# A two-layer diffusion block on one core: five weight fetches behind the softening, and a first chunk's columns ahead of the second half of its turning

## The chip, the cores and the metric

The kernel runs on one core of a Trainium2 chip. Five engines of that core take part, each with its own queue of instructions: TensorE (PE in the profile; PEld are its weight loads), VectorE (DVE), ScalarE (ACT), GpSimd (POOL) and SyncE (SP, which only starts transfers here). They wait for each other through semaphores. The metric is the device time of one execution in microseconds (us), lower is better.

## The reference

Two layers act on 256 latent tokens (`x`) and 256 context tokens (`ctx`) of width 1024, in 32-bit floats. Every layer computes shifts, scales and gates from two condition vectors, mixes the tokens, normalizes, and applies a squared-ReLU MLP of width 4096. Layer 0 mixes by retention with four heads, layer 1 by attention with 32 heads of 32 channels: a latent token attends to a window of 4 rows by 16 columns of latent tokens, with a bias for each head, and to all context tokens.

```python
for i in range(DEPTH):
    mod = (silu_c @ ada_w[i] + ada_b[i])[:, None, :]
    sh1, sc1, g1, sh2, sc2, g2 = jnp.split(mod, 6, axis=-1)
    h = x * (1.0 + sc1) + sh1              # and hc from ctx
    y, yc = retention_mixer(...) if i % 2 == 0 else neighbourhood_mixer(...)
    x = layer_norm(DN_ALPHA * x + g1 * y, ...)
    x = layer_norm(DN_ALPHA * x + g2 * sq_relu_mlp(x * (1.0 + sc2) + sh2, ...), ...)
...
s = jnp.concatenate([s_loc + bias, s_ctx], axis=-1)      # in neighbourhood_mixer
prob = jax.nn.softmax(s, axis=-1)
```

## The kernel before

Matrix products keep more than one rounding's accuracy: an operand is split into a high part (`hi`, a cast on ACT) and a low part (`lo`, the difference, on DVE), and a product is the sum of three passes on PE: high by high, high by low and low by high. `fetch(n)` starts the transfer of the next n weight blocks (128x1024 each, 512 KB, into four `raw` buffers) and casts their high part on ACT; `lows(n)` forms the low parts that are still owed on DVE. `take(n)` hands the next blocks to a product. Five `hi` and five `lo` buffers go round.

In the two places that the change touches, the order of PE, ACT and DVE is the order in which the program is written (all three are "in program order" there), so an instruction that waits holds up all that stands behind it on its engine. All instructions are recorded by one helper, so nearly every row of the profile names line 84, and work is told apart by the names of its tiles.

**The start.** Layer 0's first projections run chunk by chunk over the eight 128-wide slices of the model width. For a chunk, `chunk_sums` multiplies the condition weights (`rawq`) into one bank of the accumulator memory, `prs` (`pada` in the profile), `chunk_row` copies the sums out (`row`), `chunk_columns` turns them into columns (written to `pada` again) from which DVE makes the shifts and scales (`mod`), `chunk_turn` transposes the four token tiles (`R`), and `chunk_modulate` applies `mod` and writes `hTh` and `hTl`, the operand of the projections (`pq`, `pv`). `turn_over(n)` issues n products of a constant tile (`still`) whose result nobody uses.

**The attention of layer 1.** Thirteen steps n = 0 to 12, each of which works on three groups of four heads at once, follow a table, `STEPS`, with one row (early, late, last, before, after) for each:

```python
for n, (early, late, last, before, after) in enumerate(STEPS):
    gather(n + 1); turned(n)
    fetch(early); lows(early)
    scores(n + 2); soften(n + 2)
    fetch(late); lows(late)
    run(before)
    flip(n + 1); invert(n + 2); fetch(last); attend(n)
    run(after)
```

(here with several calls to a line). `scores` is 12 products on PE into four banks (`pqk`). `soften` adds the bias and takes the minimum on DVE (`s`, `mn`, shown as ISA or CUSTOM_DVE), four instructions, and ACT follows with four exponentials (`s<-s,mn`). `before` is a projection of later heads: `K(g)` for keys (`pn`, evicted to `kT` by ACT and then DVE), `Q(2)` for queries (`pn`, evicted to `qT`), `V(t)` for values (`pnv`). `V(0)` takes four weight blocks and goes through them in order, 6 of its 24 products for each block. `flip` is 13 transposes (`ppt`), copied out by ACT and DVE in turn (`pt`). `attend` is 26 products into `pav`, which DVE multiplies with the inverted sums (`rt`) and ACT and DVE split (`oTh`, `oTl`). `turned` is a copy of a part of `pav` to `rt` on ACT. GpSimd copies a corner (`gather`) and starts the bias transfers of two steps later.

Of the kernel before, what the change touches and what calls it, by code (L numbers as in the profile page):

```python
# [104 lines left out]
def kernel(  # L105
# [46 lines left out]
    def nm(s):  # L152
        uid[0] += 1
        return f"{s}_{uid[0]}"

    def bank(s="ps"):
        return psp.tile([P, 512], F32, tag="ps", name=nm(s))
# [8 lines left out]
    def tsl(t):  # L166
        return slice(t * P, (t + 1) * P)
# [613 lines left out]
    class Weights:  # L781


        Q, V = slice(0, DK), slice(DK, DK + DV)
# [22 lines left out]
    def turn_over(n):  # L807
        for _ in range(n):
            pe.matmul(pq[0][:, :256], lhsT=still[:, :P], rhs=still[:, :256], start=True, stop=True)
# [42 lines left out]
    prs, pts, rows = {}, {}, {}  # L852
# [16 lines left out]
    def chunk_row(k, cols=slice(0, 2 * P)):  # L869
        if cols.start == 0:  # L870
            rows[k] = smp.tile([P, 256], F32, tag="row", name=nm("row"), bufs=1)
        dve.tensor_copy(out=rows[k][:, cols], in_=prs[k][:, cols])

    def chunk_columns(k):
        for i in range(2):
            pe.matmul(
                prs[k][:, 2 * i : 2 * i + 2], lhsT=rows[k][:, tsl(i)], rhs=cv("sel4")[:, 0:2],
                start=True, stop=True,
            )
        dve.tensor_add(  # L880
            out=mods[0, 0][:, :, k, :],
            in0=prs[k][:, 0:4].rearrange("p (s t) -> p s t", s=2),
            in1=bcol[:, :, k].unsqueeze(2).broadcast_to([P, 2, 2]),
        )

    KINDS = slice(0, NLAT), slice(NLAT, NT)

    def chunk_turn(k):

        pts[k] = bank("pt")[:, 0:256], prs[k][:, 256:512]  # L890
        for t in range(4):
            pe.transpose(pts[k][t // 2][:, tsl(t % 2)], R[t][:, tsl(k)], ident)

    def modulated(e, out_ap, pt, k, a):
# [47 lines left out]
    turn_over(3)  # L942
    chunk_sums(0, 1)
    chunk_row(0, tsl(1))
    chunk_turn(0)
    chunk_columns(0)
    turn_over(4)
    w = ws[0]
    w.high(w.Q)
    chunk_modulate(0, lambda: (w.high(w.V), w.low(w.Q)))  # L950
# [6 lines left out]
    for k in range(KC):  # L957
# [10 lines left out]
        if k < KC - 1:  # L968
            for i in range(2):
                chunk_sums(k + 1, i)  # L970
            chunk_turn(k + 1)
            ws[k + 1].high()
            chunk_row(k + 1)
            if k > 2:
                ws[k + 1].low()
# [69 lines left out]
    for h in range(RH):  # L1045
# [13 lines left out]
        else:  # L1059
# [7 lines left out]
            for u in range(4):  # L1067
                ((wh, wl),) = take(1)
                for t in range(4):
                    for kk in range(2):  # L1070
                        k = 2 * u + kk
# [431 lines left out]
    def q_pair(p):  # L1503
        for u in range(2):
            q_mm(p, u)
        q_evac(p)
# [20 lines left out]
    def k_part(g, a=0, b=NT):  # L1527
        k_evac(k_mm(g, a, b), g, a, b)
# [11 lines left out]
    def v_part(half, t):  # L1540
        if t == 0:
            vu[0] = take(4, 0)
        ps = bank("pnv")
        for k in range(KC):
            wh, wl = vu[0][k // 2]
            mm3(ps[:], hs(k, t * P, (t + 1) * P), (wh[:, k % 2, :], wl[:, k % 2, :]), k == 0, k == KC - 1)
        act.copy(out=vtile(t, half), in_=ps[:])
# [28 lines left out]
    sums, rrs, Es, pts, pss = {}, {}, {}, {}, {}  # L1576
# [245 lines left out]
    def K(g):  # L1822
        return lambda: k_part(g)

    def Q(p):
        return lambda: q_pair(p)

    def V(t):
        return lambda: v_part(1, t)

    def W(half, t):
# [7 lines left out]
    REST = lambda: rest_evac(rest_mm(1))  # L1839
    STEPS = [  # L1840
        (1, 0, 0, [K(2)], []),
        (2, 0, 0, [K(3)], []),
        (2, 0, 0, [K(4)], []),
        (1, 0, 0, [K(5)], []),
        (2, 0, 0, [Q(2)], []),
        (1, 1, 0, [V(0)], []),
        (0, 0, 0, [V(1)], []),
        (0, 0, 0, [V(2)], [REST]),
        (0, 0, 0, [V(3)], []),
# [399 lines left out]
```

## Time and profile before

| what | value |
|---|---|
| median of 3 runs | 1186.27 us (1185.79 to 1186.78) |
| profiled execution | 1188.31 us, of which span 1186.5 us |
| PE busy | 1176.7 us, 99% of the span |
| DVE busy | 832.8 us, 70% |
| ACT busy | 480.9 us, 41% |
| POOL busy | 248.9 us, 21% |
| transfers | 193.16 MB, mean 163 GB/s |

The profile is of one execution; its engines' busy shares are averages over stages with different limits. PE's 99% counts a product as busy until its modelled end, so short waits inside a stage show only in the rows of that stage. The start takes the first 10 us, the steps of the attention lie between 848 and 960 us.

### The profile page before, as it was taken

To read this page: it belongs to the slowest core of one execution; us is meant where nothing else is said; L and a number is where in the kernel's file an instruction comes from. 1 tells how busy PE (TensorE), PEld (TensorE's weight loads), DVE (VectorE), ACT (ScalarE), POOL (GpSimd) and SP (SyncE) were. 2 spreads that over 40 slices of the span, in tenths; PEclk is the share of its full clock that TensorE was granted. 3 is DMA by queue.
4 is the path that set the end of the run, shared out by engine and by line. 5 is a ranking of instruction groups with operands and counts; after the bars stand their busy time and mean duration, and the time that the engine had idled before them with its cause. 6 is when DMAs were issued, how large, how long until landed. Compare 5 with 4: busy or idle time off the path is not lost.

```text
span 1186.5 us, 17867 instructions
## 1 busy us (share of the span) xinstructions
PE 1176.7 (99%) x6884; PEld 990.9 (84%) x6884; DVE 832.8 (70%) x1304; ACT 480.9 (41%) x813; POOL 248.9 (21%) x389
## 2 busy tenths in 40 slices
PE   9999999999999999999999999999999999999997
PEld 7778888888888889888888888889888878999886
DVE  3876975886688487757876675668467588876446
ACT  3652222322223246441212333137466666665341
POOL 0104301310330141780202000223344430000001
PEclk9999999999999999999999999999999999999999
DMA  9964441444254216756566665637244434765660
GB/s 276 273 234 161 142 158 56 143 130 137 89 160 160 77 55 209 203 112 215 177 193 211 200 213 185 206 108 215 69 143 125 118 122 152 224 201 185 227 212 36
DMA packets 138041, 193.16 MB, mean 163 GB/s; under 512 B 9772, under 2 KB 81108, under 8 KB 137956
## 3 DMA queue, kind: packets, MB, share of 16 engines
q1 hardware_dynamic: 129572, 179.02, 47.3%
q0 software_dynamic: 7232, 10.44, 3.9%
q10 hardware_dynamic: 1152, 2.56, 0.7%
q8 instruction: 54, 0.88, 0.3%
q14 instruction: 31, 0.25, 0.1%
HBM read 187.15 MB, written 5.75 MB: 163 GB/s over the span
## 4 chain that ended last, share of the span: by engine, by line
PE 96%; ACT 1%; DVE 1%; issue 1%; DMA 0%; POOL 0%; DVEq 0%; ACTq 0%
PE p L84 44%; PE pq L84 8%; PE pg L84 7%; PE pv L84 7%; PE pw L84 7%; PE pn L84 5%; PE pnv L84 4%; PE po L84 3%; PE pada L84 2%; PE pnw L84 1%; PE pS L84 1%; PE ppt L84 1%; PE pqk L84 1%; PE pt L84 1%; PE pav L84 1%; PE p1t L84 1%
## 5 line engine op out<-in xcount | busy, mean ns | idle before, releaser
L84 ACT CAST hi<-raw 128x1024 fp32r<-128x1024 f32 (+2 forms) x228 | 232.7, 1032 | 325.0 <-PE p L84 151.3
L84 DVE TENSOR_TENSOR lo<-raw,hi 128x1024 fp32r<-128x1024 f32 (+2 forms) x228 | 280.3, 1240 | 101.8 <-ACT hi L84 101.0
L84 PE MATMUL p<-hi,hid 128*128 128x512 f32 (+1 forms) x832 | 241.8, 374 | 0.0
L84 PEld LDWEIGHTS p<-hi,hid 128*128 128x128 f32 x832 | 152.1, 188 | 27.7
L84 PE MATMUL p<-hTh,lo 128*128 128x256 f32 (+1 forms) x512 | 166.9, 329 | 0.0
L84 PE MATMUL p<-hTl,hi 128*128 128x256 f32 (+1 forms) x512 | 166.9, 329 | 0.0
L84 PE MATMUL p<-hTh,hi 128*128 128x256 f32 (+1 forms) x512 | 164.0, 330 | 0.0
L84 PE MATMUL p<-lo,hid 128*128 128x512 f32 (+1 forms) x416 | 155.3, 373 | 0.0
L84 DVE SCALAR_TENSOR_TENSOR acc<-rawa,scol,acc 128x1024 f32<-128x1024 f32 x56 | 74.7, 1344 | 63.1 <-DMA rawa<-in_ada_w_dram 62.9
L84 POOL TENSOR_TENSOR R<-R,acc 128x512 f32<-128x512 f32 x40 | 62.2, 1565 | 212.3 <-DVE acc L84 212.2
L84 PEld LDWEIGHTS p<-hTl,hi 128*128 128x128 f32 x512 | 96.4, 188 | 8.7
L84 PEld LDWEIGHTS p<-hTh,lo 128*128 128x128 f32 x512 | 96.3, 188 | 8.8
L84 PEld LDWEIGHTS p<-hTh,hi 128*128 128x128 f32 x512 | 95.1, 190 | 8.7
L84 PEld LDWEIGHTS p<-lo,hid 128*128 128x128 f32 x416 | 78.4, 188 | 13.6
L84 ACT CAST hid<-r 128x256 fp32r<-128x256 f32 (+1 forms) x64 | 31.9, 500 | 103.4 <-DVE r L84 103.3
L84 DVE SCALAR_TENSOR_TENSOR strips<-rawa,scol,strips 128x512 f32<-128x512 f32 x84 | 66.4, 847 | 0.0
L84 POOL TENSOR_TENSOR rstd<-rstd,misc 128x1 f32<-128x1 f32 x28 | 19.2, 686 | 215.5 <-DVE rstd L84 214.3
L84 ACT ACTIVATE s<-s,mn 128x512 f32<-128x512 f32 x64 | 45.5, 712 | 26.2 <-DVE mn L84 26.1
L84 PE MATMUL pg<-hi,hTh 128*128 128x512 f32 x128 | 51.1, 399 | 0.0
L84 PE MATMUL pw<-hi,oh 128*128 128x512 f32 x128 | 50.9, 398 | 0.0
L84 PE MATMUL pg<-lo,hTh 128*128 128x512 f32 x128 | 50.0, 391 | 0.0
L84 PE MATMUL pw<-hi,ol 128*128 128x512 f32 x128 | 50.0, 390 | 0.0
(238 smaller groups left out, 2277.1 us busy)
## 6 DMA issues: line engine op xcount, KB each, us to landing
raw<-in_mlp_w_dram SPq DMA_DIRECT2D x128, 512.0 KB, 4.2
rawa<-in_ada_w_dram SPq DMA_DIRECT2D x80, 512.0 KB, 4.3
raw<-in_ret_w_in_dram SPq DMA_DIRECT2D x42, 512.0 KB, 3.6
raw<-in_nat_w_in_dram SPq DMA_DIRECT2D x24, 512.0 KB, 3.9
rawq<-in_ada_w_dram SPq DMA_DIRECT2D x16, 512.0 KB, 5.8
raw<-in_ret_w_o_dram SPq DMA_DIRECT2D x16, 512.0 KB, 4.4
bias<-rpb_rows POOLq DMA_DIRECT2D x32, 128.0 KB, 2.9
raw<-in_nat_w_o_dram SPq DMA_DIRECT2D x8, 512.0 KB, 4.1
```

The source lines that it names most:

```text
L84: r = f(*args, **kwargs)
```

## The change

In the first chunk, the second pair of the transposes (context tokens, `R_105`) goes into a bank of its own instead of the second half of `prs`, and stands behind `chunk_columns`; one of the four idle products behind it is dropped. In steps 1 to 5 of the attention, the blocks that `fetch(early)` and `lows(early)` handled ahead of the softening are handled by `fetch(late)` and `lows(late)` behind it. Step 5 had one block on either side; now both are behind. The number of blocks in each step, and every product, stay the same.

```diff
-    def chunk_turn(k):
+    def chunk_turn(k, ts=range(4)):
 
-        pts[k] = bank("pt")[:, 0:256], prs[k][:, 256:512]
-        for t in range(4):
+        if k not in pts:
+            pts[k] = bank("pt")[:, 0:256], (prs[k][:, 256:512] if k else bank("pt")[:, 0:256])
+        for t in ts:
             pe.transpose(pts[k][t // 2][:, tsl(t % 2)], R[t][:, tsl(k)], ident)
...
-    chunk_turn(0)
+    chunk_turn(0, (0, 1))
     chunk_columns(0)
-    turn_over(4)
+    chunk_turn(0, (2, 3))
+    turn_over(3)
...
         (1, 0, 0, [K(2)], []),
-        (2, 0, 0, [K(3)], []),
-        (2, 0, 0, [K(4)], []),
-        (1, 0, 0, [K(5)], []),
-        (2, 0, 0, [Q(2)], []),
-        (1, 1, 0, [V(0)], []),
+        (0, 2, 0, [K(3)], []),
+        (0, 2, 0, [K(4)], []),
+        (0, 1, 0, [K(5)], []),
+        (0, 2, 0, [Q(2)], []),
+        (0, 2, 0, [V(0)], []),
         (0, 0, 0, [V(1)], []),
```

PE at the start of the program, around the first chunk's columns (`pada_177<-cst_81,row_186`; `cst_81` holds the identity):

```order
 L84 MATMUL pada_177<-rawq_121,cT 32x128 x8
 L84 MATMUL pt_205<-cst_81,R_104 128x128 x2
-L84 MATMUL pada_177<-cst_81,R_105 128x128 x2
 L84 MATMUL pada_177<-cst_81,row_186 128x2 x2
-L84 MATMUL pq_116<-still_95 128x256 x4
+L84 MATMUL pt_206<-cst_81,R_105 128x128 x2
+L84 MATMUL pq_116<-still_95 128x256 x3
 L84 MATMUL pq_116<-hTh,hi_217 128x512
```

The columns moved ahead of the second pair of transposes, whose result is now `pt_206`.

ACT in step 5 (`oTh_6957<-rt_7687` ends step 4; the four ACTIVATE are the exponentials; the two casts are the high parts of the last block of `V(0)` and of the first block of `Q(3)`), before:

```order
L84 CAST oTh_6957<-rt_7687 128x4x32
L84 COPY rt_7834<-pav_6956 128x128
L84 CAST hi_7838<-raw_7836 128x1024
L84 ACTIVATE s_7860,sums_7859<-s_7860,mn_7858 128x512
L84 ACTIVATE s_7863,sums_7859<-s_7863,mn_7858 128x512
L84 ACTIVATE s_7866,sums_7859<-s_7866,mn_7858 128x512
L84 ACTIVATE s_7869,sums_7859<-s_7869,mn_7858 128x512
L84 CAST hi_7874<-raw_7872 128x1024
```

and of the change:

```order
L84 CAST oTh_6957<-rt_7687 128x4x32
L84 COPY rt_7834<-pav_6956 128x128
L84 ACTIVATE s_7854,sums_7853<-s_7854,mn_7852 128x512
L84 ACTIVATE s_7857,sums_7853<-s_7857,mn_7852 128x512
L84 ACTIVATE s_7860,sums_7853<-s_7860,mn_7852 128x512
L84 ACTIVATE s_7863,sums_7853<-s_7863,mn_7852 128x512
L84 CAST hi_7868<-raw_7866 128x1024
L84 CAST hi_7873<-raw_7871 128x1024
```

The high part of `V(0)`'s last block (`hi_7838`, now `hi_7868`) went from ahead of the four exponentials to behind them.

DVE behind the softening of step 4, where two blocks are handled and the queries are evicted (`qT`), before:

```order
L84 ISA s_7728,mn_7717<-pqk_7704,bias_6872 128x512
L84 ISA mn_7717 128x1
L84 SCALAR_TENSOR_TENSOR qT_6611<-pn_7731,qT_6611 128x256
L84 SCALAR_TENSOR_TENSOR qT_6611<-pn_7732,qT_6611 128x256
L84 COPY pt_6960<-ppt_7790 128x384
```

and of the change:

```order
L84 ISA mn_7705 128x1
L84 TENSOR_TENSOR lo_7722<-raw_7719,hi_7721 128x1024
L84 TENSOR_TENSOR lo_7727<-raw_7724,hi_7726 128x1024
L84 SCALAR_TENSOR_TENSOR qT_6611<-pn_7731,qT_6611 128x256
L84 SCALAR_TENSOR_TENSOR qT_6611<-pn_7732,qT_6611 128x256
L84 COPY pt_6960<-ppt_7790 128x384
```

The two low parts now stand between the softening and the eviction of the projection, and no longer ahead of the softening.

## The prediction

> **What bounds the kernel now.** I read the page first, then the chain of work that ended last in order of time around the attention's steps, then the rows of DVE, ACT and PE there, and last the first 30 us.
>
> ```profile
> span 1186.5 us, 17867 instructions
> ...
> PE 96%; ACT 1%; DVE 1%; issue 1%; DMA 0%; POOL 0%; DVEq 0%; ACTq 0%
> ```
>
> PE carries 96% of the chain, so only work that makes PE wait can be worth time. In the steps it does wait. In the chain the columns are start, length and what:
>
> ```profile
> 857.69 0.90 PE pqk L84 x10
> 858.59 5.67 PE pn L84 x24
> ...
> 875.93 0.47 ACT kT L84
> 876.40 0.38 ACT pt L84
> ...
> 876.82 1.31 PE pqk L84 x9
> ...
> 883.84 1.42 PE ppt L84 x13
> 885.26 1.12 PE pav L84 x27
> 886.39 1.28 PE pqk L84 x12
> 887.67 5.95 PE pn L84 x48
> ...
> 896.16 1.64 PE pqk L84 x11
> ...
> 906.02 1.53 PE pqk L84 x11
> ...
> 915.77 0.90 PE pqk L84 x9
> ```
>
> A step in which PE waits for nothing is 0.90 scores + 5.67 projection + 1.42 transposes + 1.12 attend = 9.11 us. Step 1 starts at 857.69, so without a wait step 3's scores would start at 875.91 and last 0.90, to 876.81. They ended at 876.82 + 1.31 = 878.13: 1.32 lost by then. In steps 4, 5 and 6 the scores took 1.28, 1.64 and 1.53 in place of 0.90: 0.38, 0.74 and 0.63 lost. From 915.77 on (step 7) nothing is. All that the steps can give is therefore 1.32 + 0.38 + 0.74 + 0.63 = 3.07 us, 0.26% of the whole. What held the scores back is a bank that ACT and DVE had not emptied (ACT's `kT` and `pt` stand right ahead in the chain), so the loop through these two engines was longer than PE's 9.11.
>
> **That loop, before and after.** DVE's rows (start, length, what), then ACT's:
>
> ```profile
> 858.53 0.29 DVE L84 TENSOR_TENSOR oTl<-rt,oTh 128x128 fp32r<-128x128 f32 x1 [0.37 <-ACT oTh L84]
> ...
> 866.14 0.69 DVE L84 TENSOR_TENSOR kT<-pn,kT 128x512 fp32r<-128x512 f32 x1 [1.70 <-ACT kT L84]
> 866.75 1.15 DVE L84 COPY pt<-ppt 128x384 f32<-128x384 f32 x2
> ...
> 868.88 0.29 DVE L84 TENSOR_TENSOR oTl<-rt,oTh 128x128 fp32r<-128x128 f32 x1 [0.37 <-ACT oTh L84]
> 869.99 2.36 DVE L84 TENSOR_TENSOR lo<-raw,hi 128x1024 fp32r<-128x1024 f32 x2 [0.82 <-ACT hi L84]
> ...
> 876.43 0.69 DVE L84 TENSOR_TENSOR kT<-pn,kT 128x512 fp32r<-128x512 f32 x1 [1.63 <-ACT kT L84]
> ...
> 896.04 0.75 DVE L84 SCALAR_TENSOR_TENSOR qT<-pn,qT 128x256 fp32r<-128x256 f32 x2 [1.44 <-ACT qT L84]
> 896.71 1.14 DVE L84 COPY pt<-ppt 128x384 f32<-128x384 f32 x2
> ...
> 905.72 1.23 DVE L84 TENSOR_TENSOR lo<-raw,hi 128x1024 fp32r<-128x1024 f32 x1 [2.10 <-ACT hi L84]
> 906.86 1.15 DVE L84 COPY pt<-ppt 128x384 f32<-128x384 f32 x2
> ...
> 908.99 0.29 DVE L84 TENSOR_TENSOR oTl<-rt,oTh 128x128 fp32r<-128x128 f32 x1 [0.37 <-ACT oTh L84]
> 909.30 0.69 DVE L84 CUSTOM_DVE_ANT_1 s<-pqk,bias 128x512 f32<-128x512 f32 x1
> ```
>
> ```profile
> 868.91 2.00 ACT L84 CAST hi<-raw 128x1024 fp32r<-128x1024 f32 x2
> ...
> 901.82 0.73 ACT L84 ACTIVATE s<-s,mn 128x512 f32<-128x512 f32 x1 [1.90 <-DVE mn L84]
> ...
> 904.66 1.03 ACT L84 CAST hi<-raw 128x1024 fp32r<-128x1024 f32 x1
> ...
> 910.04 0.72 ACT L84 ACTIVATE s<-s,mn 128x512 f32<-128x512 f32 x1 [0.92 <-DVE mn L84]
> ```
>
> Before, a round with two blocks took 876.43 - 866.14 = 10.29 us. The change reorders it; each link is a distance of two starts above. From the keys' eviction to `oTl`: 868.88 - 866.14 = 2.74. From `oTl` to a softening that stands right behind it: 909.30 - 908.99 = 0.31. From there to the first exponential: 910.04 - 909.30 = 0.74. Four exponentials: 904.66 - 901.82 = 2.84. From a cast to its low part: 905.72 - 904.66 = 1.06. A low part, to the next on DVE: 906.86 - 905.72 = 1.14. The second cast adds nothing, since two take 2.00 and its low part has to wait for the first one anyway. So a round with two blocks becomes 2.74 + 0.31 + 0.74 + 2.84 + 1.06 + 2 x 1.14 = 9.97, and with one block 8.83. The work is the same; it is only 0.32 shorter, because the casts, which DVE waited for ahead of the softening, now stand behind the exponentials, and DVE waits for them there.
>
> Rounds after the change, from the `oTl` of 858.53, which lies ahead of the first moved row: softening at 858.84; the keys' eviction of step 1 at 858.84 + 6.92 = 865.76 (before 866.14); step 2 at + 9.97 = 875.73 (before 876.43); step 3, one block, at + 8.83 = 884.56; the queries' eviction of step 4 at + 9.97 = 894.53 (before 896.04). PE follows: steps 2 to 4 run nearly at 9.11, and the banks turn so that the scores of step 3 no longer wait for the keys' bank. In step 5 two of the four banks still come from `qT`, whose pair takes 0.75: 894.53 + 0.75 = 895.28, then nine score products of 0.90 / 12 each, and `V(0)` starts near 896.0, against 896.16 + 1.64 = 897.80. So some 1.8 of the 2.44 lost ahead of it come back.
>
> **Where it is given back.** `V(0)`'s last block (products 19 to 24) was cast ahead of the softening; now it is cast behind step 5's exponentials, in the very step that uses it. Its low part: 894.53, eviction to `oTl` 2.74 + 0.06 (the queries' pair takes 896.71 - 896.04 = 0.67 where the keys take 866.75 - 866.14 = 0.61), softening at 897.64, cast 0.74 + 2.84 later at 901.22, low part 902.28 to 903.51 (1.23). PE before:
>
> ```profile
> 902.17 0.39 PE L84 MATMUL pnv<-lo,hTh 128*128 128x512 f32 x1
> ...
> 903.32 1.47 PE L84 MATMUL ppt<-cst,s 128*128 128x128 f32 x12
> ```
>
> The first product with this low part (number 20) started at 902.17, so PE reached it 902.17 - 897.80 = 4.37 into `V(0)`; after, it arrives at 896.0 + 4.37 = 900.4 and stands until 903.55: a new wait of 3.2 us, more than was won. From there it runs 903.55 - 902.17 = 1.38 late. Behind it stand the transposes and attend of step 5 and all later steps. ACT and DVE, who wait for PE there, get a lead: step 6's scores need banks that are emptied during the transposes, so their 0.63 goes. Net of the steps: 1.38 - 0.63 = +0.75 us.
>
> Ends: if a link on each round is 0.2 longer (two late transfers, two semaphores), five rounds put 1.0 on this; if PE arrives later or the casts sooner by as much, 1.0 comes off: -0.25 to +1.75. The eight moved blocks' transfers keep their order on SP, whose queue holds nothing else there, and the low parts that free their buffers come a step or more ahead of the next cast; POOL's bias transfers start behind the exponentials, which come earlier, and are used two steps later: I take nothing for both.
>
> **The start.**
>
> ```profile
> 8.66 0.29 DVE L84 COPY row<-pada 128x128 f32<-128x128 f32 x1 [0.92 <-PE pada L84]
> ...
> 9.01 0.44 PE L84 MATMUL pada<-cst,R 128*128 128x128 f32 x2
> ...
> 9.28 0.51 PE L84 MATMUL pada<-cst,row 128*128 128x2 f32 x4
> ...
> 9.82 0.16 DVE L84 TENSOR_TENSOR mod<-pada,bcol 128x4 f32<-128x4 f32 x1 [0.87 <-PE pada L84]
> 10.02 0.57 ACT L84 ACTIVATE hTh<-pt,mod 128x256 fp32r<-128x256 f32 x1 [0.60 <-DVE mod L84]
> ...
> 22.01 0.83 ACT L84 CAST hi<-raw 128x768 fp32r<-128x768 f32 x1 [4.46 <-DMA raw<-in_ret_w_in_dram]
> ...
> 22.90 0.57 ACT L84 ACTIVATE hTh<-pt,mod 128x256 fp32r<-128x256 f32 x1
> ```
>
> The columns start where the transposes did, 9.28 - 9.01 = 0.27 earlier, and so does `mod`; DVE's half of `hTh` then waits for the transposes behind the columns, which leaves about 0.2. The dropped idle product lies in PE's wait for `hTh` and costs nothing. But chunk 2's cast waits for its transfer until 22.01 and ends at 22.84, 0.06 ahead of `hTh` at 22.90: of the 0.2, at most 0.06 survives. I take -0.04 (ends -0.2, if that transfer lands earlier, and +0.1).
>
> **Sum.** +0.75 - 0.04 = +0.7 us. The profiled execution's 1188.31 (its span and 1.81 around it), which is 2.04 over the median, would be 1189.0; on the median, 1186.27 + 0.7 = 1187.0 us. That is 0.06%, within the 0.2% (2.4 us) that a measurement of this kernel can about tell from no change.
>
> **Rivals.** *The last block comes in time* (faster). All 3.07 and the start's 0.2 are gained: 1183.0. For it: each round is shorter. Against: the low part would have to be done at 900.4 and not 903.5, and nothing in the rows shortens DVE's and ACT's loop by 3 us in four rounds. It decides from a gain of 2.4: with the 0.6 that step 5's scores still wait, 3.07 + 0.2 - 0.6 leaves `V(0)` a wait of 0.3 us at most. *PE falls back to its slow pace in the new wait* (slower).
>
> ```profile
> 1.23 3.78 PE pq L84 x16
> ```
>
> At the program's start a 256-wide product takes 3.78 / 16 = 0.236 us; in `Q(2)` 5.95 / 48 = 0.124. The first products of a program run at half pace for some 5 us, though the granted clock reads full there. If the wait of 3.2 us in step 5 brings that back for as long, 2.5 us are lost on top: 1189.5. It decides when the wait counts as rest; the rows of before have no wait of this length behind which one could look, and here product 19 (high by high) breaks it 1.2 us ahead of its end. [...] *The loop stays as long as it was* (10.29, so `qT` still at 896.04): then the low part ends 1.51 later, +2.2 in all, 1188.5.
>
> **Chances.** Forecast, between -0.25 and +1.75: 0.70. Loop as before: 0.10, half of it over the bound. Half pace: 0.08. In time: 0.06, and a part of the way there, -2.4 to -0.25, 0.06. So faster 0.06, same 0.70 + 0.06 + 0.05 = 0.81, slower 0.13. Eight in ten lie between 1185.4 (the forecast's low end and the spread of the runs) and 1188.7 (the loop as before).
>
> **What would show it.** Right: `V(0)` starts near 896.0 and holds a wait of about 3 us for the last block's `hi` and `lo`; rounds of DVE near 9.97 and 8.83; scores of step 6 near 0.90; step 7 some 0.7 later than 915.77. Wrong: `V(0)` without a wait, or products behind it at 0.4 us distance instead of 0.23, or chunk 2's `hTh` 0.2 ahead of 22.90.

## The result

| | kernel before | changed kernel |
|---|---|---|
| median | 1186.71 us (14 executions, 1185.75 to 1188.81) | 1188.81 us (14 executions, 1187.20 to 1192.90) |
| profiled execution | 1188.31 us, span 1186.5 us | 1188.83 us, span 1186.9 us |
| mean clock in the profiled execution | 0.999 | 0.997 |

The ratio of after to before is 1.002, with a 95% interval of 1.0012 to 1.0029: the change costs about 2.1 us (by the interval 1.4 to 3.4 us). The forecast was +0.7 us and a range up to 1188.7, which the median misses by 0.1 us. The direction and the place were right, the size was not.

The loop through DVE and ACT did what was worked out. DVE's rows of the changed kernel (start, length, what):

```profile
866.35 0.68 DVE L84 TENSOR_TENSOR kT<-pn,kT 128x512 fp32r<-128x512 f32 x1
...
876.32 0.68 DVE L84 TENSOR_TENSOR kT<-pn,kT 128x512 fp32r<-128x512 f32 x1
...
885.16 0.68 DVE L84 TENSOR_TENSOR kT<-pn,kT 128x512 fp32r<-128x512 f32 x1
...
895.12 0.75 DVE L84 SCALAR_TENSOR_TENSOR qT<-pn,qT 128x256 fp32r<-128x256 f32 x2
...
902.87 2.36 DVE L84 TENSOR_TENSOR lo<-raw,hi 128x1024 fp32r<-128x1024 f32 x2 [2.11 <-ACT hi L84]
```

The rounds are 9.97, 8.84 and 9.96 us (9.97, 8.83 and 9.97 were expected), and the last block's low part begins 0.59 us behind the 902.28 of the prediction. Those 0.59 are already there in the row ahead of the first moved one (`oTl` at 859.12 instead of 858.53), so they come from earlier in the program. Then the new wait, in PE's rows:

```profile
900.85 0.39 PE L84 MATMUL pnv<-hi,hTl 128*128 128x512 f32 x1
902.88 0.50 PE L84 MATMUL pnv<-hi,hTh 128*128 128x512 f32 x1 [1.64 <-ACT hi L84]
904.14 0.73 PE L84 MATMUL pnv<-lo,hTh 128*128 128x512 f32 x1 [0.76 <-DVE lo L84]
904.67 0.63 PE L84 MATMUL pnv<-hi,hTl 128*128 128x512 f32 x1
905.10 0.63 PE L84 MATMUL pnv<-hi,hTh 128*128 128x512 f32 x1
...
906.38 2.10 PE L84 MATMUL ppt<-cst,s 128*128 128x128 f32 x12
```

Product 19 waits 1.64 us for its high part, product 20 another 0.76 for its low part, as foreseen. In all product 20 starts about 2.8 us later than its turn (901.31, by the usual 0.23 from 900.85); 3.2 were expected, because PE got there 0.3 us later than worked out. What was not foreseen as likely comes behind it: the products stand 0.43 us apart instead of 0.23. The view by stretches of time shows the granted clock in the column PEclk. The stretches here are 3.41 us long:

```profile
core 0: us, PE busy (x) PEld busy (x) DVE busy (x) ACT busy (x) POOL busy (x), PEclk, DMA share, GB/s
897.42:900.83 3.41, 3.41 (x16) 2.80 (x15) 2.95 (x10) 2.34 (x7) 0.60 (x2) 1.00 0.41 128
900.83:904.24 3.41, 1.01 (x4) 0.28 (x2) 1.38 (x2) 2.95 (x6) 3.37 (x9) 1.00 0.36 102
904.24:907.66 3.42, 3.42 (x12) 2.83 (x13) 0.98 (x1) 0.99 (x2) 1.22 (x3) 0.50 0.84 217
907.66:911.07 3.41, 3.41 (x49) 2.64 (x49) 2.46 (x7) 1.02 (x4) 0.00 (x0) 1.00 0.42 147
```

From 904.24 to 907.66 the granted clock reads 0.50. At half pace 3.42 us hold the work of 1.71, an estimate from that reading. In the chain of the changed kernel this is the difference between the pieces behind the wait and the usual ones (1.42 for the transposes):

```profile
898.96 2.94 ACT s L84 x8
901.90 0.94 ACT hi L84
902.87 1.24 DVE lo L84
904.14 2.44 PE pnv L84 x5
906.58 2.01 PE ppt L84 x13
...
909.72 0.90 PE pqk L84 x7
```

I measure the steps from the first score product of step 0 to that of step 7. Before, that is 915.70 - 848.51 = 67.19 us, after, 918.77 - 849.07 = 69.70:

```profile
849.07 0.98 PE L84 MATMUL pqk<-kT,qT 32*128 32x512 f32 x12
918.77 0.97 PE L84 MATMUL pqk<-kT,qT 32*128 32x512 f32 x12
```

So the steps lost 2.51 us, though the two profiled executions differ by only 0.5. The profiled execution of before lost time elsewhere. In the chain, the same 1104 products of the last stage, without a wait among them, took 162.12 us before:

```profile
1016.92 162.12 PE p L84 x1104
```

and 159.35 us after:

```profile
1020.09 159.35 PE p L84 x1104
```

Three of the 14 profiled executions of this study show the longer time (one of each of three kernels: before, the changed one when it ran a second time, and a third one below), so it belongs to the execution and not to the change. The account of the two spans: +0.56 ahead of step 0, +2.51 in steps 0 to 7, +0.29 from there to about 1000 us, -0.19 up to the 1104 products, -2.77 in them, in all +0.40 (1186.9 - 1186.5).

### The profile page after: what moved, and what is told of

The parts are those of the page before. It is cut to its first block, busy times and chain, and to the rows that moved or that the text cites. A ratio compares the mean times of both kernels' runs of the same rounds, so it can differ in the third digit from the quotient of the medians.

```text
span 1186.9 us, 17863 instructions
## 1 busy us (share of the span) xinstructions
PE 1174.5 (99%) x6883; PEld 988.0 (83%) x6883; DVE 833.2 (70%) x1304; ACT 480.3 (40%) x813; POOL 249.4 (21%) x389
## 4 chain that ended last, share of the span: by engine, by line
PE 89%; DMA 3%; DVE 3%; ACT 2%; issue 1%; SPq 1%; POOL 1%; ACTq 0%; DVEq 0%; POOLq 0%
PE p L84 43%; PE pg L84 7%; PE pw L84 7%; PE pv L84 6%; PE pq L84 6%; PE pnv L84 4%; PE pn L84 3%; PE po L84 3%; PE pnw L84 2%; PE pS L84 1%; PE ppt L84 1%; SPq L84 1%; PE pav L84 1%; ACT s L84 1%; PE pt L84 1%
```

## The experiments

Each kernel was timed beside the kernel before on the same chip. "Steps" is the distance from step 0's scores to step 7's in the profiled execution; "halved" says where the clock reads 0.50 in that stretch.

| kernel | steps, us | halved, us | median, us (range) | ratio to before, 95% |
|---|---|---|---|---|
| before | 67.19 | no | 1186.71 (1185.75 to 1188.81) | |
| changed | 69.70 | 904.24 to 907.66 | 1188.81 (1187.20 to 1192.90) | 1.0012 to 1.0029 |
| steps alone | 70.00 | 904.81 to 908.22 | 1188.97 (1187.66 to 1192.83) | 1.0008 to 1.0029 |
| start alone | 66.82 | no | 1186.84 (1185.61 to 1190.30) | 0.9988 to 1.0010 |
| step 5 as before | 65.65 | no | 1185.78 (1184.75 to 1189.10) | 0.9983 to 1.0004 |
| idle products | 68.02 | no | 1189.95 (1187.56 to 1191.66) | 1.0010 to 1.0030 |
| changed, second time | 69.68 | 906.26 to 909.67 | 1190.41 (1188.85 to 1192.66) | 1.0017 to 1.0041 |
| step 5 alone | 70.89 | 906.35 to 909.76 | 1190.37 (1189.89 to 1196.12) | 1.0020 to 1.0047 |
| step 5 with one block | 65.08 | no | 1185.42 (1184.41 to 1190.73) | 0.9976 to 1.0002 |
| the same, step 0 late too | 67.98 | no | 1188.80 (1188.05 to 1194.33) | 1.0009 to 1.0030 |
| changed, third time | 69.57 | 905.30 to 908.71 | 1190.01 (1187.10 to 1196.18) | 1.0015 to 1.0041 |
| idle products, second time | 68.04 | no | 1188.90 (1187.08 to 1193.85) | 1.0002 to 1.0026 |
| one block, second time | 65.05 | no | 1184.89 (1183.78 to 1187.42) | 0.9972 to 0.9990 |
| one block, start as before | 65.44 | no | 1185.72 (1183.91 to 1191.19) | 0.9981 to 1.0003 |

Below the changed kernel the table has three groups of four kernels. Each group shared its own runs of the kernel before, with medians of 1187.02, 1187.04 and 1187.10 us.

**Steps alone, start alone.** The change has two parts that do not touch each other in the program. Steps alone:

```diff
-    chunk_turn(0, (0, 1))
+    chunk_turn(0)
     chunk_columns(0)
-    chunk_turn(0, (2, 3))
-    turn_over(3)
+    turn_over(4)
```

> The table of steps as changed, the start as before. Theory A (PE's clock is halved behind the wait in step 5, in some executions): all of the loss is in the steps, so this stands with the changed kernel, some executions near 1187.2 us (clock kept, the wait alone, +0.7 on the kernel before) and some near 1188.8 (3.4 us at half pace, +1.7 more), products 20 to 24 of V(0) 0.45 apart in the profile where the clock reads 0.5. Theory B (the extra is lost at the start, where the changed kernel fell 0.57 us behind before 100 us): 0.6 or more below the changed kernel's 1188.8 in the same kind of execution, so 1188.2 at most, and attention begins 0.57 earlier.

Start alone:

```diff
-        (0, 2, 0, [K(3)], []),
-        (0, 2, 0, [K(4)], []),
-        (0, 1, 0, [K(5)], []),
-        (0, 2, 0, [Q(2)], []),
-        (0, 2, 0, [V(0)], []),
+        (2, 0, 0, [K(3)], []),
+        (2, 0, 0, [K(4)], []),
+        (1, 0, 0, [K(5)], []),
+        (2, 0, 0, [Q(2)], []),
+        (1, 1, 0, [V(0)], []),
```

> The start as changed, the table of steps as before. Theory A: 1186.7 us, within 0.3 of the kernel before, clock 0.999 in all executions, since the transfers set the pace until 37 us. Theory B: 1187.3 to 1188.0, and waits for transfers of 0.2 to 0.3 us between 30 and 80 us again, which the kernel before doesn't have.

Theory A holds: the steps alone are as slow as the whole change, the start alone is level with before. Theory B falls, also by its own mark: with the start as before, step 0 began at 849.07 too. When step 0 begins lies between 848.51 and 850.63 over all profiled executions, with either start, and a part of it is lost on transfers. In the execution of the start alone PE stood 1.4 us for one (this view lists PE's waits: in total, how often, longest):

```profile
PE pada L84 <- DMA rawa<-in_ada_w_dram: 1.4, 1, 1.4
```

**Step 5 as before**, in the changed kernel:

```diff
-        (0, 2, 0, [V(0)], []),
+        (1, 1, 0, [V(0)], []),
```

> The changed kernel with step 5's row as before: V(0)'s last block is cast ahead of the softening again, steps 1 to 4 keep their blocks behind it. Theory A: the four shorter rounds bring V(0) to some 1.8 us earlier (897.80 to 896.0 by the kernel before's times), no wait in V(0), clock 0.999 in all executions; step 6 still waits about 0.6. 1186.7 - 1.8 = 1184.9 us (1184.3 to 1185.5). Rival: the late casts in steps 1 to 4 cost something themselves (their transfers or bias transfers later, rounds not shorter): 1186.7 or more.

The steps take 65.65 us, 1.54 less than before, so the four shorter rounds do pay. The wait is gone from `V(0)`, and step 6 still waits 1.49 - 0.90 = 0.6 as expected:

```profile
895.72 1.53 PE pqk L84 x10
897.25 5.71 PE pnv L84 x24
...
905.50 1.49 PE pqk L84 x11
```

The median is 1.2 us under that of before, but the interval of the ratio still reaches over 1, and 1185.78 is above the expected 1185.5.

**Idle products in the wait.** Twelve products of 256 columns ahead of product 19 and four ahead of product 20 give PE work while it waits; their result is overwritten unused.

```diff
+    def keep_warm(n):
+        hh = hTh[:, 0, 0:P], hTh[:, 0, 0 : 2 * P]
+        for _ in range(n):
+            pe.matmul(av_half(5), lhsT=hh[0], rhs=hh[1], start=True, stop=True)
...
+            if (half, t, k) == (1, 0, 6):
+                keep_warm(12)
+                ah, al = hs(k, 0, P)
+                pe.matmul(ps[:], lhsT=ah, rhs=wh[:, 0, :], start=False, stop=False)
+                keep_warm(4)
+                pe.matmul(ps[:], lhsT=ah, rhs=wl[:, 0, :], start=False, stop=False)
+                pe.matmul(ps[:], lhsT=al, rhs=wh[:, 0, :], start=False, stop=False)
+                continue
```

> The changed kernel with 12 idle products of 256 columns ahead of V(0)'s product 19 and 4 ahead of product 20 (result unused, some 1.4 and 0.5 us of PE, both shorter than the waits there). The wait for the last block stays as it is. Theory A (idleness halves the clock): no execution loses its clock, products 20 to 24 at 0.23, all executions near 1187.3 us with clock 0.999, 1.5 below the changed kernel's median. Rival C (the slow products behind the wait come from the transfers that run there, DMA share 0.9 to 1.0 at 905 to 909 us, or from reading a low part just written): products 20 to 24 still 0.45 apart, 1188.8 us.

> The changed kernel with the idle products in the waits of step 5. Steps 0 to 7 in 68.0 us (as before with these products), clock never halved there. Its profile agreed the first time, but its timed executions were as long as the changed kernel's. Theory A: 0.6 to 1.5 us below the changed kernel on the same chip in the median. Rival D (the idle products cost elsewhere what they save, or the halved clock is not what the timed executions lose): no difference in the median.

This separates the wait from what follows it. PE's rows of the first of these kernels:

```profile
901.16 1.59 PE L84 MATMUL pav<-hTh 128*128 128x256 f32 x12
903.01 0.50 PE L84 MATMUL pnv<-hi,hTh 128*128 128x512 f32 x1 [0.26 <-ACT hi L84]
903.35 0.64 PE L84 MATMUL pav<-hTh 128*128 128x256 f32 x4
904.27 0.50 PE L84 MATMUL pnv<-lo,hTh 128*128 128x512 f32 x1 [0.29 <-DVE lo L84]
904.61 0.40 PE L84 MATMUL pnv<-hi,hTl 128*128 128x512 f32 x1
904.84 0.40 PE L84 MATMUL pnv<-hi,hTh 128*128 128x512 f32 x1
```

Product 20 still waits for its low part (904.27), and behind it the products stand 0.23 us apart. The chain of the second time has 1.41 and 1.42 where the changed kernel has 2.44 and 2.01:

```profile
902.78 1.24 DVE lo L84
904.02 0.04 issue
904.06 1.41 PE pnv L84 x5
905.47 1.42 PE ppt L84 x13
```

The steps take 68.02 and 68.04 us against 69.70, 69.68 and 69.57: the half pace costs 1.6 us. With the idle products PE was busy for 2.95 us from 900.77 to 904.18 (the first of these kernels) and for 3.03 from 900.50 to 903.91 (the second), and the clock stayed at 1.00; in the changed kernel it was busy for 1.01 of the 3.41 us, and the clock fell. So here PE's idleness brings the half pace on. Rival C falls: in the stretch behind the wait the same transfers run at a DMA share of 0.84, product 20 reads a low part just written, and the clock (1.00) is kept. In the second of these kernels that stretch is:

```profile
903.91:907.33 3.42, 3.27 (x29) 2.90 (x33) 2.19 (x4) 1.45 (x3) 1.46 (x3) 1.00 0.84 189
```

In time the result is less clean. The first time the median was 1189.95, a miss by 2.6 us; the second time, beside the changed kernel on one chip, 1188.90 against 1190.01, the 1.1 us that theory A allows, but the two kernels' own spreads are wider than that. What the longer of these executions lose is open. A halved stretch in each of them is unlikely: the mean clock is 0.998 or 0.999 in all 24, while 20 of 33 executions of the changed kernel have 0.997 or less (below), and five of the longer ones (over 1190 us) here have 0.999. So the profiles show what the half pace costs in the steps, but the medians do not show that the whole of it comes back when the clock is kept, and they do not rule out rival D.

**The changed kernel again, twice.** These two show in which executions, and when, the clock is halved.

> The changed kernel once more, unaltered, beside the others on one chip. Theory A (PE's clock is halved for 3.4 us when a window of 3.4 us, counted on a raster that does not follow the program, holds too little work): steps 0 to 7 (from scores to scores) take 69.7 us in an execution in which the clock is halved near 904 us and 68.0 in one in which it is not; some executions have a mean clock of 0.999 and the others 0.997, and the first are about 1.7 us faster. Where the profile shows a halving at 904 us, it lies a whole number of 3.413 us before the halving at the program's end. Rival (the halving always follows the wait): every execution has the clock of 0.997.

> The changed kernel, beside the next one on one chip. Steps 0 to 7 take 69.7 us if PE's clock is halved behind the wait in step 5 in the profiled execution, 68.0 if not; where it is, the halving lies a whole number of 3.413 us before the one behind PE's last product, and PE is busy for less than about half of the 3.41 us ahead of it.

All profiled executions with the wait in `V(0)` and without the idle products (three of the changed kernel, one of the steps alone, one of step 5 alone) were halved, at different distances from the end of the wait. In each, the same clock reading falls to 0.50 once more behind PE's last product. In the first profile these two moments are 904.24 and 1184.14, which is 279.90 us or 82.0 times 3.413; the others give 82.0, 82.0, 82.0 and 81.0. The halving in the steps is 3.413 us long in the clock record of the changed kernel and 3.41 in the views of the other four. So in these five traces the two falls of the clock lie a whole number of 3.413 us apart. They do not lie at a fixed distance from the end of the wait: the first comes 0.10, 0.37, 0.96 and 1.25 us behind the start of product 20 (the changed kernel, the steps alone, step 5 alone, the changed kernel's second time), and the third time 0.13 us ahead of it. With step 5 alone (below) the products at 905.72, 905.96 and 906.19 still stand 0.23 to 0.24 us apart, and the clock falls at 906.35. The third time, the stretches counted from the fall at 905.30 were:

```profile
898.48:901.89 3.41, 3.41 (x17) 2.80 (x16) 3.03 (x10) 2.11 (x7) 0.37 (x2) 1.00 0.50 161
901.89:905.30 3.41, 1.09 (x4) 0.36 (x2) 1.31 (x4) 3.17 (x6) 3.36 (x9) 1.00 0.32 83
905.30:908.71 3.41, 3.28 (x10) 2.69 (x11) 1.21 (x2) 0.69 (x2) 1.43 (x3) 0.50 0.83 196
908.71:912.12 3.41, 3.41 (x51) 2.64 (x50) 2.31 (x7) 1.32 (x4) 0.00 (x0) 1.00 0.53 188
```

One stretch with PE busy for 1.09 of 3.41 us has the whole of the next at half clock. Over the three groups, 20 of 33 executions of the changed kernel had a mean clock of 0.997 or less and 13 of 0.998 or more; their medians are 1190.26 and 1188.10 us, their lowest times 1188.72 and 1187.10. Of the executions of the kernel before that ran beside the experiments (97) none had less than 0.998. That fits a clock that falls behind this wait in some executions and not in others; an execution of the changed kernel without the halving was not caught by the profiler. A mean of 0.998 doesn't settle a single execution, since the profiled one of the steps alone has it with a halving.

**Step 5 alone late**, steps 1 to 4 as before. The text below says that the start is as before, which is wrong: this kernel has the changed start.

```diff
-        (0, 2, 0, [K(3)], []),
-        (0, 2, 0, [K(4)], []),
-        (0, 1, 0, [K(5)], []),
-        (0, 2, 0, [Q(2)], []),
+        (2, 0, 0, [K(3)], []),
+        (2, 0, 0, [K(4)], []),
+        (1, 0, 0, [K(5)], []),
+        (2, 0, 0, [Q(2)], []),
```

> The kernel before (start and steps 1 to 4), with step 5's row alone changed: V(0)'s last block is cast behind the softening. The loop stays at 10.29 us, so the keys' and queries' evictions stay and the low part of that block is ready some 2.9 us after PE needs it. Theory A: steps 0 to 7 take 67.2 + 2.9 - 0.6 = 69.5 us with the clock kept and 71.2 with it halved; 1189.0 or 1190.7 us. Together with the run that has step 5 as before (65.65) it gives the whole change's 68.0 without a halved clock, so the two parts add up. Rival (a casting order in steps 1 to 4 is what costs): 67.2, as before.

The steps take 70.89 us with the clock halved, against an expected 71.2, and the median is 1190.37. PE's rows:

```profile
904.13 0.50 PE L84 MATMUL pnv<-hi,hTh 128*128 128x512 f32 x1 [1.69 <-ACT hi L84]
905.39 0.50 PE L84 MATMUL pnv<-lo,hTh 128*128 128x512 f32 x1 [0.76 <-DVE lo L84]
905.72 0.40 PE L84 MATMUL pnv<-hi,hTl 128*128 128x512 f32 x1
905.96 0.40 PE L84 MATMUL pnv<-hi,hTh 128*128 128x512 f32 x1
906.19 0.49 PE L84 MATMUL pnv<-lo,hTh 128*128 128x512 f32 x1
906.48 0.63 PE L84 MATMUL pnv<-hi,hTl 128*128 128x512 f32 x1
```

and the stretches counted from the fall of its clock:

```profile
902.94:906.35 3.41, 1.47 (x5) 1.01 (x6) 2.24 (x2) 2.08 (x4) 3.22 (x7) 1.00 0.52 126
906.35:909.76 3.41, 3.41 (x17) 3.11 (x16) 0.68 (x2) 1.54 (x3) 0.53 (x1) 0.50 0.96 266
```

The parts add up, each taken from one profiled execution. From the start alone (66.82): late casts in steps 1 to 4 give 65.65 - 66.82 = -1.17; step 5's late cast gives 70.89 - 66.82 = +4.07, of which 1.6 is the half pace. Together that is 69.72, and 69.70 was measured.

**Step 5 with one block.** V(0)'s last block ahead of step 5's softening, the other block behind step 6's:

```diff
-        (0, 2, 0, [V(0)], []),
-        (0, 0, 0, [V(1)], []),
+        (1, 0, 0, [V(0)], []),
+        (0, 1, 0, [V(1)], []),
```

> The changed kernel, but step 5 fetches only V(0)'s last block, ahead of its softening, and the other block (Q(3)'s first, used four steps later) goes behind the softening of step 6. No wait in V(0), clock kept. With step 5 as before, steps 0 to 7 took 65.65 us, of which step 6's scores waited 0.6, since step 5's loop held a second low part (1.14) behind the softening. That wait goes: 65.05 us in the steps, 2.1 below the kernel before: 1184.6 if the kernel before stands at 1186.7. Rival: the block moved to step 6 makes step 7 wait instead, 65.6.

> Step 5 fetches only V(0)'s last block, ahead of its softening, the other block goes behind the softening of step 6. As measured: 65.1 us in steps 0 to 7, 2.1 less than the kernel before, of which 0.3 is given back by 1000 us: 1.6 to 1.8 below the kernel before in the median. Rival (the difference was one chip's spread): within 0.5 of it.

> The same steps with the start as before. If the start is worth nothing: the same time within 0.4 and again 1.6 to 1.8 below the kernel before. If the changed start saves its 0.2 us or costs by the transfers behind it: 0.2 more, or 0.5 and more less, than with the changed start.

The steps came out at 65.08 and 65.05 us where 65.05 was expected. Step 6's scores no longer wait, in the second execution's chain:

```profile
896.86 5.67 PE pnv L84 x24
...
905.08 0.91 PE pqk L84 x8
```

The second time the median was 1184.89 against 1187.10 us, ratio 0.9981 (0.9972 to 0.9990): this version is faster than the kernel before, by 1.2 to 3.3 us, and than the changed one. The first time the interval just reached 1 (0.9976 to 1.0002). With the start as before, the steps take 65.44 and the median is 1185.72 (0.9981 to 1.0003); whether the start makes that difference is not settled, since the profiled one of these is the third execution with the long 162.12 us in the last stage. One of its 12 executions had a mean clock of 0.995 (1191.19 us) though `V(0)` does not wait in the profiled one, so a mean below 0.998 can also come from elsewhere; where it was lost is not known.

**Step 0 late too**:

```diff
-        (1, 0, 0, [K(2)], []),
+        (0, 1, 0, [K(2)], []),
```

> The same with step 0's block behind the softening too. One more round shorter by 0.32 us, and step 5's scores, which still wait 0.6 for the queries' banks, by as much: 64.75 us in the steps, 1184.3. Rival: the first rounds have slack, and nothing changes (65.05).

Both expectations failed: the steps take 67.98 us, 2.9 more. Step 0's block is the second half of what `K(2)` needs in that same step, which I had not looked up, so it is the wait of step 5 over again:

```profile
856.38 0.50 PE L84 MATMUL pn<-hTh,hi 128*128 128x512 f32 x1 [1.82 <-ACT hi L84]
...
857.64 0.50 PE L84 MATMUL pn<-hTh,lo 128*128 128x512 f32 x1 [0.52 <-DVE lo L84]
```

The clock of this execution falls behind PE's last product, at 1183.84. In stretches of 3.413 us counted back from there (95.0 of them to 859.57) the two parts of the wait fall into two different ones, and the clock was kept:

```profile
852.75:856.16 3.41, 1.81 (x8) 1.14 (x7) 1.51 (x6) 3.41 (x9) 1.91 (x6) 1.00 0.09 16
856.16:859.57 3.41, 2.67 (x10) 1.91 (x11) 1.23 (x1) 0.17 (x1) 1.26 (x3) 1.00 0.69 181
```

Most of the others probably did not: 8 of the 11 executions have a mean clock of 0.997 or less.

## Why the prediction was wrong

**Right: the loop and the wait.** The rounds came to within 0.01 us, `V(0)` was held by the high and the low part of its last block as worked out, step 6's wait of 0.63 went (0.90 for its scores in the chain). The net of the steps without the half pace, +0.75 in the prediction, measured 68.02 - 67.19 = +0.83 with the idle products. That it comes so near is partly luck, since this kernel also has the changed start, with which the steps are about 0.3 us shorter (below). With the start as before, the steps alone took 70.00, which without 1.6 for the half pace is +1.2 by estimate: there the round with one block took 885.48 - 876.29 = 9.19 us instead of 8.83.

**Wrong: that the clock is kept.** The step that failed is the rival "PE falls back to its slow pace", which got a chance of 0.08 on the ground that product 19 breaks the wait, and so no term in the sum. Product 19 does break the wait, but PE was still busy for only 1.01 of 3.41 us, and the clock read 0.50 in the next stretch. Executions with the halved clock lose 1.5 to 1.7 us more there (69.57 to 69.70 against 68.03), and by the mean clock they are some 20 in 33, so the median is most likely one of these. With the term, 0.75 + 1.6 = 2.4 us on the median of before; the measured difference is 2.1. This sum fits the median but is not proved by it: the kernel with the idle products kept its clock and was yet 1.8 and 2.9 us above before in its medians, for a reason that is not known. The price that the prediction gave for the rival by the start's slow pace (2.5) was too high, since the half pace lasted one stretch of 3.41 us and not 5. Its remark that the granted clock reads full at the start misreads the view: the trace of before has no clock record until 6.6 us, and the view prints 1.00 where there is none. Of the start that trace shows the pace alone, 0.236 us a product against 0.124.

That product 19 would keep the clock was the author's estimate, and no run shows it. Here waits of 2.40 to 2.45 us in two pieces, with product 19 between them, were each followed by half clock: the stretches in which PE was busy for 0.98, 1.01, 1.09, 1.47 and 1.75 us of 3.41 have one that reads 0.50 behind them, those with 1.81 and 2.67 (step 0 late too) do not. So what went with the fall behind these waits is not whether the wait is broken but how little PE was busy in one stretch of that length.

**Right for another reason: the start.** -0.04 was predicted, and the start alone is level (1186.84 against 1187.02, interval 0.9988 to 1.0010). As foreseen, little of the earlier columns was left by chunk 2's `hTh` (22.81 instead of 22.90). Two later effects were not foreseen. With the changed start the steps are about 0.3 us shorter (66.82 against 67.19, 69.70 against 70.00, 65.05 against 65.44), and the stretch from step 7's scores to about 1000 us is longer (84.14 to 84.22 us in all eleven profiles with it, 83.88 to 83.94 in the three without). They cancel. The bank that the start takes more moves later tiles of the accumulator memory into other banks (in the built programs the first two banks of the first scores, `pqk`, are numbers 1 and 4 before and 6 and 3 after); that this is the cause was not tested.

**The chances.** The forecast's 0.81 for a difference within 0.2% took in what was measured (1.002, on the border), but the measured 2.1 us lies above the bounds of -0.25 to +1.75, which had been given 0.70.

## What to carry to other kernels

An average of the clock over a run hides a halving that lasts 3.4 us (0.997 in the mean of the changed kernel, 0.50 from 904.24 to 907.66): read the clock in stretches of that length behind every place where PE newly waits about as long as here, broken or not (the waits behind which the clock fell came to 2.40 to 2.45 us), and take the 1.5 to 1.7 us that it cost here as an estimate of the price. When fetches are moved behind a long operation, check for each block whether the same step uses it: seven of the eight moved blocks could wait, and with the eighth left in its place (and one other block a step later) a loss of 2.1 us became a gain of 1.6 us (its interval just reaching no change) and, the second time, of 2.2.

## What the runs showed of the hardware

In five profiles PE's clock read 0.50 for 3.41 us behind a stretch of 3.41 us in which PE was busy for 0.98 (the steps alone), 1.01, 1.09 and 1.75 (the changed kernel, the third and the second time) and 1.47 us (step 5 alone). Behind stretches with 1.81 and 2.67 us (step 0 late too) it read 1.00. These figures give no border: at the end of the program of before a stretch with 1.67 us of short products (1177.36 to 1180.78) passed at 1.00, and so did the next. So busy time as the profile models it does not settle alone where the clock falls.

The same 1104 products, without a wait among them, took 159.33 to 159.35 us in eleven profiled executions and 162.12 in three, with nothing between. In the profiles of before (162.12) and of the changed kernel (159.35) the clock reads 1.00 throughout them, and all of the difference lies in the products of `hTh` and `hTl`, before about 1090 us: each of them lasts 281 ns in the one and 276 ns in the other, and behind them the means agree (390 and 391 ns for 512 columns, 282 and 283 for 256). The changed kernel shows both times. What sets the one or the other is not seen in these traces.
